# Latent attention: queries of a pair of heads behind the preceding pair's keys

## The chip, the cores and the metric

One core of a Trainium2 chip runs the whole kernel. PE is TensorE, DVE VectorE, ACT ScalarE, POOL GpSimd and SP SyncE; each takes its instructions in the order in which they stand in its queue. ACT and SP also issue DMAs. The metric is the device time of one execution in microseconds; lower is better. Before the change it is 2350.18 us (median of three runs, 2349.92 to 2350.8).

## What is computed

A decoder trunk of two layers over 512 tokens of 1024 channels, in float32. Each layer has three branches beside each other (a state-space mixer, multi-head latent attention, a gated delta net), merges them with gates, and ends with a feed-forward block. The change lies in latent attention:

```python
def mla_mixer(cq, ckv, k_rope, cos, sin, q_norm_g, w_uq, kv_norm_g, w_ukv):
    q = (rmsnorm(cq, q_norm_g) @ w_uq).reshape(Bsz, S, H, MLA_NOPE + MLA_ROPE)
    q_nope, q_pe = jnp.split(q, [MLA_NOPE], axis=-1)
    q_pe = apply_rope(q_pe, cos[:, :, None, :], sin[:, :, None, :])
    kv = (rmsnorm(ckv, kv_norm_g) @ w_ukv).reshape(Bsz, S, H, MLA_NOPE + MLA_V)
    k_nope, v = jnp.split(kv, [MLA_NOPE], axis=-1)
    k_pe = apply_rope(k_rope, cos, sin)
    ...
        sc = (jnp.einsum('bqhd,bkhd->bhqk', qn, k_nope, preferred_element_type=jnp.float32)
              + jnp.einsum('bqhr,bkr->bhqk', qp, k_pe, preferred_element_type=jnp.float32))
        ...
        pr = jax.nn.softmax(sc, axis=-1)
        return jnp.einsum('bhqk,bkhd->bqhd', pr.astype(v.dtype), v)
```

There are 8 heads; a query latent of 512 channels and a key latent of 256; per head 128 channels without and 64 with rotation, and 128 value channels.

## The kernel before

Every float32 product is made of three matmuls: each operand is split into a high part (a cast on ACT) and a low part (a subtraction on DVE), and `mm3` (L181 to L183) adds high times high, high times low and low times high. Names that end in h and l are these parts: whi and wlo of a weight, cqh and cql of the query latent, ckh and ckl of the key latent.

The latent attention of a layer runs like this. `latent` takes the query latent and then the key latent: sums of squares on ACT (L491), a power on POOL (L265), scaling on DVE (L495), transposes on PE into a bank of PSUM (L500), and the eviction into high and low parts with the gain (`split_gain`, L260 on ACT and L261 on DVE). `rope` turns a tile by its angles: four DMAs that swap halves (L513), issued by ACT, then cosine, sine and sum on DVE (L515 to L517). The rotated key goes into kph and kps. Then a loop goes over four pairs of heads. For each pair it makes:
- the queries: weights (casts L552 and L553, low parts L554 and L555), a dense product with the query latent (cq) into three banks, the evictions qh and ql (`head_tiles`, L568 and L569) and qp (L575), the rope of qp, two DMAs that swap the halves of the two heads (L580), and the tiles qps and qpl. Of qps one half is a cast of the rope's sum (L584), the other a cast of what the DMAs of L580 brought (L586).
- the keys and values from the key latent (ck): kh and kl, and the values vh and vl (evicted by `split_act`, L256 on ACT and L257 on DVE), 128 tokens at a time.
- for each head the scores (L617 to L622, of which L620 reads qps), the maximum (L626), the exponential (L629), the division (L630, L631), transposes of the probabilities (L639), their eviction (tiles mix and pt, L256 and L257) and the product with the values (L655 to L657). The result goes into the tiles y.

PSUM has four banks for dense products (acc), three small ones (sm, for scores and transposes) and one for the result of a head (y, named yt in the rows). A scheduler sets the order of each engine's queue when the kernel is built, by dependences, priorities (`tc.high_priority`) and free buffers; the order in which the code is written counts, and buffers of one name are reused in turn. After the first pair the small step sizes of the state-space branch are made (`step_sizes`). In the lists below numbers behind names are those of buffers, and waits names the semaphores an instruction waits for.

Of the kernel before, what the change touches and what calls it, by code (L numbers as in the profile page):

```python
# [11 lines left out]
F32R = mybir.dt.float32r  # L12
# [3 lines left out]
ALU = mybir.AluOpType  # L16
# [4 lines left out]
P = 128  # L21
S = 512
# [37 lines left out]
def hybrid_kernel(ctx, tc, a, out, depth=2, taps=None):  # L60
    nc = tc.nc
    pe, act, dve, pool, sync = nc.tensor, nc.scalar, nc.vector, nc.gpsimd, nc.sync
    uid = itertools.count()

    def mk(pl, shape, dt, tag, bufs=None):
        return pl.tile(shape, dt, tag=tag, name=f"{tag}_{next(uid)}", bufs=bufs)

    def tap(name, ap):
        if taps and name in taps:
            sync.dma_start(taps[name], ap)  # L70

    def f32(ap):
        return ap.bitcast(F32)
# [12 lines left out]
    lp = ctx.enter_context(tc.tile_pool(name="lp", bufs=1))  # L86
# [7 lines left out]
    def y_bank():  # L94
        return mk(ps_sm, [P, 512], F32, "yt", 1)

    def sm_bank():
        return mk(ps_sm, [P, 512], F32, "sm")
# [64 lines left out]
    def weights(w2d, c0, n, K, hold=None):  # L163

        kt = min(1024 // n, K // P)
        step = 512 // n
        for k0 in range(0, K // P, kt):  # L170
            raw = mk(wp, [P, kt * n], F32, "wraw", 2)
            sync.dma_start(raw.rearrange("p (k n) -> p k n", n=n),
                           w2d[k0 * P : (k0 + kt) * P, c0 : c0 + n].rearrange("(k p) n -> p k n", p=P))
            for q in range(0, kt, step):
                hi, lo = split_half(raw[:, q * n : (q + step) * n], hold and hold[k0 + q])
                v = lambda x: x.rearrange("p (k n) -> p k n", n=n)
                yield k0 + q, v(hi), v(lo)
# [76 lines left out]
    def split_act(hi, lo, src):  # L254
        with tc.high_priority(30):
            act.copy(hi, src)  # L256
            dve.tensor_tensor(lo, src, f32(hi), ALU.subtract)  # L257
# [78 lines left out]
    for ly in range(depth):  # L336
# [5 lines left out]
        sconv_b, g_n1, g_ssd, g_q, g_kv, g_gdn, g_n2 = 0, 12, 20, 28, 32, 34, 35  # L342
# [28 lines left out]
        ps = sm_bank()  # L371
# [113 lines left out]
        def latent(tok, width, gi, nm):  # L485

            nk = width // P
            ss = mk(sp, [P, T], F32, "lss")
            for t in range(T):
                jk = mk(ml, [P, width], F32, "pn3", 2)  # L490
                act.activation(jk, tok[t], AF.Square, accum_out=ss[:, t : t + 1])  # L491
            rs = mk(sp, [P, T], F32, "lrs")
            rsq(rs, ss, 1.0 / width, EPS)
            for t in range(T):
                dve.tensor_scalar(tok[t], tok[t], rs[:, t : t + 1], None, ALU.mult)  # L495
            hs, ls = hilo_tags(ml, nm, nk)
            for k in range(nk):
                ps = sm_bank()
                for t in range(T):
                    pe.transpose(ps[:, t * P : (t + 1) * P], tok[t][:, k * P : (k + 1) * P], ident)  # L500
                split_gain(hs[k], ls[k], ps, col(gi + k))
            return hs, ls
# [1 line left out]
        ck_tok = [mk(lp, [P, 256], F32, "mix", 8) for t in range(T)]  # L504
        dense_T(weights(w_in, O_CKV, 256, D), 256, D, xh, xl, lambda t, ps: act.copy(ck_tok[t], ps))
        cqh, cql = latent(cq_tok, 512, g_q, "cq")
        ckh, ckl = latent(ck_tok, 256, g_kv, "ck")

        def rope(src):

# [20 lines left out]
        for x in pts:  # L531
            pool.memset(f32(x[:, :P]), 0.0)

        qpl = [mk(ml, [P, S], F32R, f"qpl{j}") for j in range(2)]
        for j in range(2):
            pool.memset(f32(qpl[j][64 * (1 - j) : 64 * (1 - j) + 64]), 0.0)

        scale = (128 + 64) ** -0.5
        yh, yl = [None] * KD, [None] * KD
        for hp in range(4):  # L540
            def q_weights():
                for k0 in (0, 2):
                    raw = mk(wp, [P, 768], F32, "wraw", 2)
# [12 lines left out]
                        yield k0 + k, hi.unsqueeze(1), lo.unsqueeze(1)  # L556

            *pq, pp = dense_F(q_weights(), tiles(384), 512, cqh, cql)

            def head_tiles(pss, nm, c=None):  # L560
                res = []
                for ps in pss:
                    hi = mk(ml, [P, S], F32R, nm + "h", 3)
                    lo = mk(ml, [P, S], F32R, nm + "l", 3)
                    if c is None:
                        split_act(hi, lo, ps)
                    else:
                        act.mul(hi, ps, c)  # L568
                        dve.scalar_tensor_tensor(lo, ps, c, f32(hi), ALU.mult, ALU.subtract)  # L569
                    res.append((hi, lo))  # L570
                return res

            qs = head_tiles(pq, "q", scale)
            qp = mk(ml, [P, S], F32, "qp")
            act.mul(qp, pp, scale)  # L575
            qr = rope(qp)
# [1 line left out]
            qd = mk(lp, [P, S], F32, "mix", 8)  # L578
            for i in range(2):
                act.dma_start(qd[64 * i : 64 * i + 64], qr[64 * (1 - i) : 64 * (1 - i) + 64])  # L580
            qps = [mk(ml, [P, S], F32R, f"qps{j}") for j in range(2)]
            for j in range(2):
                half, other = (slice(64 * i, 64 * i + 64) for i in (j, 1 - j))
                act.copy(qps[j][half], qr[half])  # L584
                dve.tensor_tensor(qpl[j][half], qr[half], f32(qps[j][half]), ALU.subtract)
                act.copy(qps[j][other], qd[other])  # L586
            wkv = list(weights(a["mla_w_ukv"][ly], hp * 512, 512, 256))
            with tc.high_priority(30):
                ks = head_tiles(dense_F(wkv, [slice(0, P), slice(256, 256 + P)], 256, ckh, ckl), "k")
# [15 lines left out]
            vcols = lambda w: w.rearrange("p (h n) -> p h n", h=2)[:, :, P:]  # L605
            dense_T(wkv, 256, 256, ckh, ckl, ev, vcols)

            for j in range(2):
                qh, ql = qs[j]
                kh, kl = ks[j]  # L610
                pn = []
                for t in range(T):
                    n = max(256, (t + 1) * P)
                    tok = slice(t * P, (t + 1) * P)
                    ps = sm_bank()
                    o = ps[:, :n]
                    pe.matmul(o, qh[:, tok], kh[:, :n], start=True, stop=False)  # L617
                    pe.matmul(o, qh[:, tok], kl[:, :n], start=False, stop=False)
                    pe.matmul(o, ql[:, tok], kh[:, :n], start=False, stop=False)
                    pe.matmul(o, qps[j][:, tok], kps[:, :n], start=False, stop=False)  # L620
                    pe.matmul(o, qpl[j][:, tok], kph[:, :n], start=False, stop=False)
                    pe.matmul(ps[:, t * P : n], id_b, am_b[:, : n - t * P], start=False, stop=True)  # L622
                    n = (t + 1) * P
                    o = ps[:, :n]
                    mx = mk(sp, [P, 1], F32, "mx", 8)
                    dve.tensor_reduce(mx, o, AX.X, ALU.max, negate=True)  # L626
                    pt_ = mk(ml, [P, (t + 1) * P], F32, f"pn{t}", 2)
                    sm = mk(sp, [P, 1], F32, "sme", 8)
                    act.activation(pt_[:, :n], o, AF.Exp, bias=mx, accum_out=sm)  # L629
                    dve.reciprocal(sm, sm)  # L630
                    dve.tensor_scalar(pt_[:, :n], pt_[:, :n], sm, None, ALU.mult)  # L631
                    pn.append(pt_)
                po = y_bank()
                for kbs in ((0,), (1,), (3, 2)):
                    ps = sm_bank()
                    n = 0
                    for kb in kbs:
                        for t in range(kb, T):
                            pe.transpose(ps[:, n : n + P], pn[t][:, kb * P : (kb + 1) * P], ident)  # L639
                            n += P  # L640
                    if len(kbs) == 1:
                        th = mk(lp, [P, n], F32R, "mix", 8)
                        tl = mk(lp, [P, n], F32R, "mix", 8)
                        split_act(th, tl, ps[:, :n])
                        parts = [(kbs[0], kbs[0] * P, 0)]
                    else:

                        th, tl = pts
                        split_act(th[:, P:], tl[:, P:], ps[:, :n])
                        parts = [(2, 2 * P, 2 * P), (3, 2 * P, 0)]  # L650
                    for kb, c0, c in parts:
                        v_h, v_l = (x[:, kb, :] for x in vs[j])
                        o = po[:, c0:]
                        w = S - c0
                        pe.matmul(o, v_h, th[:, c : c + w], start=kb == 0, stop=False)  # L655
                        pe.matmul(o, v_h, tl[:, c : c + w], start=False, stop=False)
                        pe.matmul(o, v_l, th[:, c : c + w], start=False, stop=kb == T - 1)  # L657
                yh[2 * hp + j], yl[2 * hp + j] = (mk(lp, [P, S], F32R, f"y{e}{2 * hp + j}") for e in "hl")
                split_act(yh[2 * hp + j], yl[2 * hp + j], po)
                tap(f"oT{2 * hp + j}", f32(yh[2 * hp + j]))  # L660
            if hp == 0:
                dec, ndec, beta, dtq, dsk, g24 = step_sizes()
        mp.close()
# [621 lines left out]
```

## Time and profile before

| what | value |
|---|---|
| median of three runs | 2350.18 us |
| the profiled execution | 2350.16 us, its span 2348.4 us, clock 0.999 |
| latent attention, first layer | about 46 to 165 us of the span |
| latent attention, second layer | about 1208 to 1330 us |
| PE busy in 46 to 165 | 114.25 of 119.00 us |
| PE busy in 1208 to 1330 | 116.91 of 122.00 us |

A row of the timeline gives the start, the duration, the engine and line, the operation with its output and input, the shape, and in brackets the engine's idle time ahead of it and what ended that. Durations of PE overlap, since matmuls are pipelined: the distance from one start to the next tells what a matmul costs. A row of waits gives the total, the number of times and the longest.

### The profile page before, as it was taken

The numbers are of one execution on the slowest core, as the hardware profiler recorded it, in microseconds if no ns is written. First come the engines' busy times: TensorE is split into PE (matmuls) and PEld (weight loads), VectorE is DVE, ScalarE is ACT, GpSimd is POOL, SyncE is SP. The second block draws the span as 40 slices with busy tenths as digits, with TensorE's granted clock in tenths as the row PEclk, the third lists the DMA queues.
The fourth block names the chain that finished last, engine by engine and source line by source line (L and its number), as shares of the span: only waits on it lengthen the run. The fifth ranks groups of instructions, "written<-read, shape, count | busy, mean of one in ns | idle before, by whom it ended". The sixth has DMA issues, their size and how long they took to land.

```text
span 2348.4 us, 32069 instructions
## 1 busy us (share of the span) xinstructions
PE 2307.8 (98%) x11972; PEld 1896.2 (81%) x11972; DVE 1607.3 (68%) x3184; ACT 1154.4 (49%) x2305; POOL 58.5 (2%) x76
## 2 busy tenths in 40 slices
PE   8999999999999999999999999999999999999998
PEld 7787788888887888888887887888887878888886
DVE  6776756775675458767757777667766645677668
ACT  5655434533453345545656553444334534555545
POOL 0000000000000000000000000000000000000000
PEclk9999999999999999999999999999999999999999
DMA  4322232252222443233132222323422224333231
GB/s 131 91 64 72 65 97 70 79 149 73 73 63 72 143 150 102 72 125 117 46 100 78 73 72 70 93 65 106 117 81 66 62 81 161 126 111 105 90 108 45
DMA packets 194172, 215.16 MB, mean 92 GB/s; under 512 B 32352, under 2 KB 153696, under 8 KB 194016
## 3 DMA queue, kind: packets, MB, share of 16 engines
q1 hardware_dynamic: 190496, 207.87, 29.1%
q10 hardware_dynamic: 3520, 5.25, 0.9%
q8 instruction: 94, 1.54, 0.3%
q14 instruction: 62, 0.51, 0.1%
HBM read 200.50 MB, written 7.34 MB: 89 GB/s over the span
## 4 chain that ended last, share of the span: by engine, by line
PE 90%; DVE 5%; DMA 2%; ACT 1%; POOL 1%; issue 1%; SPq 0%; ACTq 0%; DVEq 0%; POOLq 0%
PE acc L181 23%; PE acc L182 23%; PE acc L183 23%; PE sm L183 2%; PE sm L181 2%; PE sm L182 2%; PE sm L735 1%; DVE wlo L160 1%; PE sm L639 1%; PE yt L182 1%; PE yt L181 1%; PE yt L183 1%; PE sm L1000 1%; PE sm L296 1%; PE sm L461 1%
## 5 line engine op out<-in xcount | busy, mean ns | idle before, releaser
L160 DVE TENSOR_TENSOR wlo<-wraw,whi 128x512 fp32r<-128x512 f32 x552 | 377.9, 688 | 401.8 <-ACT whi L159 391.8
L159 ACT CAST whi<-wraw 128x512 fp32r<-128x512 f32 x552 | 341.9, 621 | 623.6 <-PE acc L182 407.9
L181 PE MATMUL acc<-xh,whi 128*128 128x512 f32 (+1 forms) x1184 | 462.0, 391 | 0.0
L182 PE MATMUL acc<-xl,whi 128*128 128x512 f32 (+1 forms) x1184 | 459.4, 388 | 0.0
L183 PE MATMUL acc<-xh,wlo 128*128 128x512 f32 (+1 forms) x1184 | 459.0, 388 | 0.0
L182 PEld LDWEIGHTS acc<-xl,whi 128*128 128x128 f32 x1184 | 223.0, 188 | 42.5 <-issue 1.0
L183 PEld LDWEIGHTS acc<-xh,wlo 128*128 128x128 f32 x1184 | 222.9, 188 | 41.8 <-issue 0.5
L181 PEld LDWEIGHTS acc<-xh,whi 128*128 128x128 f32 x1184 | 222.8, 189 | 41.7 <-issue 0.5
L181 PE MATMUL acc<-yh,whi 128*128 128x512 f32 x384 | 153.1, 402 | 0.0
L182 PE MATMUL acc<-yl,whi 128*128 128x512 f32 x384 | 152.3, 397 | 0.0
L183 PE MATMUL acc<-yh,wlo 128*128 128x512 f32 x384 | 151.4, 394 | 0.0
L183 PE MATMUL acc<-whi,xl 128*128 128x512 f32 (+1 forms) x384 | 144.0, 375 | 0.0
L181 PE MATMUL acc<-whi,xh 128*128 128x512 f32 (+1 forms) x384 | 143.9, 376 | 0.0
L182 PE MATMUL acc<-wlo,xh 128*128 128x512 f32 (+1 forms) x384 | 143.4, 373 | 0.0
L676 DVE SCALAR_TENSOR_TENSOR cva<-acc,pc,cva 128x511 f32<-128x511 f32 (+2 forms) x168 | 120.2, 743 | 16.7 <-ACT cva L672 9.5
L159 ACT CAST whi<-wr 128x512 fp32r<-128x512 f32 x128 | 79.5, 621 | 68.3 <-PE acc L183 32.7
L181 PE MATMUL acc<-whi,yh 128*128 128x512 f32 x256 | 99.7, 390 | 0.0
L183 PE MATMUL acc<-whi,yl 128*128 128x512 f32 x256 | 99.7, 389 | 0.0
L182 PE MATMUL acc<-wlo,yh 128*128 128x512 f32 x256 | 99.6, 389 | 0.0
L160 DVE TENSOR_TENSOR wlo<-wr,whi 128x512 fp32r<-128x512 f32 x128 | 85.8, 685 | 12.6 <-ACT whi L159 12.1
L182 PEld LDWEIGHTS acc<-yl,whi 128*128 128x128 f32 x384 | 72.2, 188 | 16.1 <-issue 1.9
L181 PEld LDWEIGHTS acc<-yh,whi 128*128 128x128 f32 x384 | 71.6, 188 | 16.8 <-ACT yh L260 2.3
(409 smaller groups left out, 4597.9 us busy)
## 6 DMA issues: line engine op xcount, KB each, us to landing
wraw<-in_w_in_dram SPq DMA_DIRECT2D x148, 512.0 KB, 3.6
wraw<-in_w_up_dram SPq DMA_DIRECT2D x64, 512.0 KB, 3.7
wr<-in_w_down_dram SPq DMA_DIRECT2D x32, 1024.0 KB, 5.0
wraw<-in_w_mla_out_dram SPq DMA_DIRECT2D x16, 512.0 KB, 3.4
wraw<-in_w_ssd_out_dram SPq DMA_DIRECT2D x16, 512.0 KB, 3.4
wraw<-in_w_gdn_out_dram SPq DMA_DIRECT2D x16, 512.0 KB, 3.3
wraw<-in_w_out_dram SPq DMA_DIRECT2D x16, 512.0 KB, 3.7
wraw<-in_mla_w_uq_dram SPq DMA_DIRECT2D x16, 384.0 KB, 3.4
```

The source lines that it names most:

```text
L159: act.copy(hi, raw)
L160: dve.tensor_tensor(lo, raw, f32(hi), ALU.subtract)
L181: pe.matmul(o, ah, bh, start=start, stop=False, skip_group_check=more)
L182: pe.matmul(o, ah, bl, start=False, stop=False, skip_group_check=more)
L183: pe.matmul(o, al, bh, start=False, stop=stop, skip_group_check=more)
L296: pe.transpose(ps[:, j * P : (j + 1) * P], xr[j % 2][:, kk * P : (kk + 1) * P], ident)
L461: pe.matmul(ps, w, cum[1][:, t].rearrange("p i l -> p (i l)"), start=True, stop=True)
L639: pe.transpose(ps[:, n : n + P], pn[t][:, kb * P : (kb + 1) * P], ident)
L676: dve.scalar_tensor_tensor(acc[:, d:], ps[:, : S - d], taps_[3 - d], acc[:, d:], ALU.mult, ALU.add)
L735: pe.matmul(py[:, h * 64 : (h + 1) * 64], e2[h // 4][:, h % 4, :], xd[:, h * 64 : (h + 1) * 64], start=True, stop=True)
L1000: pe.matmul(po[:, h * P : (h + 1) * P], pt_[:, h, :], vn[:, h * P : (h + 1) * P], start=True, stop=True)
```

## The change

The body of the loop is cut into three functions: `queries`, `keys` and `attend`. The order is now queries of the first pair, the key latent, and then for each pair its keys, the next pair's queries, and its attention. So that two pairs' queries can live at once, the odd pairs' tiles use room that is free at that time: tiles of y, and of the query latent for the last pair. The idle halves of their qpl are cleared on POOL each time (4 clearings of 64x512 per layer more), and all these clearings stay in the order of the program. The fourth transposed block of the query latent goes into the bank y instead of a small one. The matmuls are the same in number and size; SP's queue has the same order as before.

```diff
             hs, ls = hilo_tags(ml, nm, nk)
             for k in range(nk):
-                ps = sm_bank()
+                ps = y_bank() if k == 3 else sm_bank()
...
         cqh, cql = latent(cq_tok, 512, g_q, "cq")
-        ckh, ckl = latent(ck_tok, 256, g_kv, "ck")
...
-        qpl = [mk(ml, [P, S], F32R, f"qpl{j}") for j in range(2)]
+        base_qpl = [mk(ml, [P, S], F32R, f"qpl{j}") for j in range(2)]
+        clean = lambda x, j: tc.keep_in_program_order(pool.memset(f32(x[64 * (1 - j) : 64 * (1 - j) + 64]), 0.0))
         for j in range(2):
-            pool.memset(f32(qpl[j][64 * (1 - j) : 64 * (1 - j) + 64]), 0.0)
+            clean(base_qpl[j], j)
...
-        for hp in range(4):
+        def head_tiles(pss, nm, c=None, homes=None):
+            res = []
+            for j, ps in enumerate(pss):
+                hi, lo = homes[j] if homes else (mk(ml, [P, S], F32R, nm + e, 3) for e in "hl")
...
+        y_home = lambda k: [mk(lp, [P, S], F32R, f"y{e}{k}") for e in "hl"]
+        cq_home = lambda k: [mk(ml, [P, S], F32R, f"cq{e}{k}") for e in "hl"]
+
+        def queries(hp):
...
-            qs = head_tiles(pq, "q", scale)
+            qs = head_tiles(pq, "q", scale, [y_home(hp * 2 + j if hp == 1 else 6 + j) for j in range(2)] if hp % 2 else None)
             qp = mk(ml, [P, S], F32, "qp")
             act.mul(qp, pp, scale)
             qr = rope(qp)
...
-            qps = [mk(ml, [P, S], F32R, f"qps{j}") for j in range(2)]
+            if hp % 2:
+                qps, qpl = zip(*((y_home if hp == 1 else cq_home)(k) for k in ((4, 5) if hp == 1 else (2, 3))))
+                for j in range(2):
+                    clean(qpl[j], j)
+            else:
+                qps, qpl = [mk(ml, [P, S], F32R, f"qps{j}") for j in range(2)], base_qpl
             for j in range(2):
                 half, other = (slice(64 * i, 64 * i + 64) for i in (j, 1 - j))
                 act.copy(qps[j][half], qr[half])
                 dve.tensor_tensor(qpl[j][half], qr[half], f32(qps[j][half]), ALU.subtract)
                 act.copy(qps[j][other], qd[other])
+            return qs, qps, qpl
+
+        def keys(hp):
...
+            return ks, vs
+
+        def attend(hp, qs, qps, qpl, ks, vs):
...
+        qq = [queries(0)]
+        ckh, ckl = latent(ck_tok, 256, g_kv, "ck")
+        for hp in range(4):
+            kv = keys(hp)
+            if hp < 3:
+                qq.append(queries(hp + 1))
+            attend(hp, *qq[hp], *kv)
             if hp == 0:
                 dec, ndec, beta, dtq, dsk, g24 = step_sizes()
```

In the new code the lines of queries are L571 to L574 (weights' casts and low parts), L548 and L549 (qh and ql), L580 (qp), L585 (the two DMAs), and L594 to L596 (own half of qps, qpl, other half of qps). The rope is L512 to L516, the scores are L634 to L639, the exponential L646, the transposes of the probabilities L656 and the clearings L531.

The first place is ACT's queue at the first pair of the first layer, where the values are evicted. Before, the eight value evictions (vh) end ahead of the first of the two DMAs L580:

```order
L256 CAST vh_854<-acc_858 128x128
L256 CAST vh_856<-acc_860 128x128 [waits DVE_49]
L552 CAST whi_1172<-wraw_1170 128x256 [waits DMAHW1_49]
L256 CAST vh_856<-acc_861 128x128 [waits DVE_49]
L256 CAST vh_856<-acc_859 128x128 [waits DVE_49]
L256 CAST vh_856<-acc_858 128x128 [waits DVE_49]
L553 CAST whi_1172<-wraw_1170 128x128
L552 CAST whi_1187<-wraw_1170 128x256
L553 CAST whi_1187<-wraw_1170 128x128
L580 DMA mix_811<-mix_807 64x512 [waits DMAHW0_49,DVE_49]
L159 CAST whi_1234<-wraw_1232 128x512 [waits DMAHW6_49,PE_49]
```

Now the row ahead of the DMAs is the third eviction of the first head:

```order
L256 CAST vh_854<-acc_860 128x128 [waits PE_49]
L571 CAST whi_939<-wraw_937 128x256 [waits DMAHW1_49,PE_49]
L585 DMA mix_777<-mix_773 64x512 [waits DMAHW7_49,DVE_49]
L585 DMA mix_777<-mix_773 64x512
L594 CAST qps_162_780<-mix_773 64x512
L594 CAST qps_163_781<-mix_773 64x512
L596 CAST qps_163_781<-mix_777 64x512 [waits DMAHW7_49]
L256 CAST vh_856<-acc_858 128x128 [waits DVE_49]
L596 CAST qps_162_780<-mix_777 64x512 [waits DMAHW1_49]
L256 CAST vh_856<-acc_859 128x128 [waits DVE_49]
L256 CAST vh_854<-acc_861 128x128 [waits PE_49]
```

The two DMAs and the four casts of qps, two of which wait for the DMAs, stand ahead of the rest of the second head's values (vh_856).

The second place is ACT's queue in the attention of the first pair, first layer, from an exponential (pn) to the evictions of transposed probabilities (mix and pt). Before:

```order
L629 ACTIVATE pn_197_911,sme_912<-sm_902,mx_909 128x128 [waits DVE_49]
L629 ACTIVATE pn_201_925,sme_926<-sm_916,mx_923 128x256 [waits DVE_49]
L629 ACTIVATE pn_205_939,sme_940<-sm_930,mx_937 128x384 [waits DVE_49]
L629 ACTIVATE pn_209_953,sme_954<-sm_944,mx_951 128x512 [waits DVE_49]
L568 ACTIVATE qh_1202<-acc_1135 128x512 [waits PE_49]
L568 ACTIVATE qh_1206<-acc_1136 128x512 [waits PE_49]
L256 CAST mix_964<-sm_959 128x512 [waits PE_49]
L256 CAST pt_149_717<-sm_982 128x384 [waits PE_49]
L256 CAST mix_975<-sm_971 128x384
```

Now, from the fourth exponential on:

```order
L646 ACTIVATE pn_234_1054,sme_1055<-sm_1045,mx_1052 128x512 [waits DVE_49]
L585 DMA mix_988<-mix_984 64x512 [waits DVE_49]
L585 DMA mix_988<-mix_984 64x512
L594 CAST yh_216_991<-mix_984 64x512
L594 CAST yh_218_993<-mix_984 64x512
L596 CAST yh_218_993<-mix_988 64x512 [waits DMAHW1_49]
L256 CAST mix_1065<-sm_1060 128x512 [waits PE_49]
L596 CAST yh_216_991<-mix_988 64x512 [waits DMAHW2_49]
L256 CAST mix_1076<-sm_1072 128x384 [waits PE_49]
L256 CAST pt_137_683<-sm_1083 128x384 [waits PE_49]
```

Between exponential and evictions now stand the two DMAs and the four casts of the second pair's qps (which live in the tiles yh_216 and yh_218), with the waits for the DMAs.

The third place is PE's queue where the scores of the second pair's first head begin (first layer). Before:

```order
L183 MATMUL acc_1506<-cqh_122_632,wlo_1542 128x512
L181 MATMUL acc_1611<-ckh_138_682,whi_1603 128x512 [waits DVE_49,Activation_49]
L181 MATMUL acc_1504<-cqh_123_633,whi_1556 128x512
L182 MATMUL acc_1611<-ckl_140_684,whi_1603 128x512
L620 MATMUL sm_1312<-kps_713,qps_281_1224 128x256 [waits Activation_49]
L621 MATMUL sm_1312<-kph_712,qpl_151_721 128x256 [waits DVE_49]
L622 LDWEIGHTS id_b_77
```

Now:

```order
L182 MATMUL acc_1318<-cql_127_637,whi_1368 128x512
L183 MATMUL acc_1318<-cqh_123_633,wlo_1369 128x512
L634 MATMUL sm_1413<-kh_1260,yh_208_969 128x256 [waits PE_49]
L635 MATMUL sm_1413<-kl_1261,yh_208_969 128x256
L636 MATMUL sm_1413<-kh_1260,yl_209_970 128x256
L637 MATMUL sm_1413<-kps_679,yh_216_991 128x256
L638 MATMUL sm_1413<-kph_678,yl_217_992 128x256 [waits Pool_49]
```

The product with qps (L620) stood first here, behind key products that lie further ahead, and waits for ACT; now the key products (L634 to L636) stand together with it, the product with qps (L637, in yh_216) has no wait of its own, and the next (L638) has one for POOL's clearing.

More of the change, by code (lines that the diff above doesn't have):

```diff
@@ L532, in hybrid_kernel @@
             pool.memset(f32(x[:, :P]), 0.0)
-        qpl = [mk(ml, [P, S], F32R, f"qpl{j}") for j in range(2)]
+        base_qpl = [mk(ml, [P, S], F32R, f"qpl{j}") for j in range(2)]
+        clean = lambda x, j: tc.keep_in_program_order(pool.memset(f32(x[64 * (1 - j) : 64 * (1 - j) + 64]), 0.0))
         for j in range(2):
-            pool.memset(f32(qpl[j][64 * (1 - j) : 64 * (1 - j) + 64]), 0.0)
+            clean(base_qpl[j], j)
         scale = (128 + 64) ** -0.5
         yh, yl = [None] * KD, [None] * KD
-        for hp in range(4):
+        def head_tiles(pss, nm, c=None, homes=None):
+            res = []
+            for j, ps in enumerate(pss):
+                hi, lo = homes[j] if homes else (mk(ml, [P, S], F32R, nm + e, 3) for e in "hl")
+                if c is None:
+                    split_act(hi, lo, ps)
+                else:
+                    act.mul(hi, ps, c)
+                    dve.scalar_tensor_tensor(lo, ps, c, f32(hi), ALU.mult, ALU.subtract)
+                res.append((hi, lo))
+            return res
+        y_home = lambda k: [mk(lp, [P, S], F32R, f"y{e}{k}") for e in "hl"]
+        cq_home = lambda k: [mk(ml, [P, S], F32R, f"cq{e}{k}") for e in "hl"]
+        def queries(hp):
             def q_weights():
@@ L558, in hybrid_kernel @@
             *pq, pp = dense_F(q_weights(), tiles(384), 512, cqh, cql)
[L560 to L571, printed above, removed]
-            qs = head_tiles(pq, "q", scale)
+            qs = head_tiles(pq, "q", scale, [y_home(hp * 2 + j if hp == 1 else 6 + j) for j in range(2)] if hp % 2 else None)
             qp = mk(ml, [P, S], F32, "qp")
@@ L580, in hybrid_kernel @@
                 act.dma_start(qd[64 * i : 64 * i + 64], qr[64 * (1 - i) : 64 * (1 - i) + 64])
-            qps = [mk(ml, [P, S], F32R, f"qps{j}") for j in range(2)]
+            if hp % 2:
+                qps, qpl = zip(*((y_home if hp == 1 else cq_home)(k) for k in ((4, 5) if hp == 1 else (2, 3))))
+                for j in range(2):
+                    clean(qpl[j], j)
+            else:
+                qps, qpl = [mk(ml, [P, S], F32R, f"qps{j}") for j in range(2)], base_qpl
             for j in range(2):
```

## The prediction

> **What bounds the kernel now.** I read first the busy shares and the chain of the page, then the waits of PE in the two latent attention stages (about 46 to 165 us and 1208 to 1330 us), then the timelines of PE, DVE and ACT there.
>
> ```profile
> span 2348.4 us, 32069 instructions
> PE 2307.8 (98%) x11972; PEld 1896.2 (81%) x11972; DVE 1607.3 (68%) x3184; ACT 1154.4 (49%) x2305; POOL 58.5 (2%) x76
> PE 90%; DVE 5%; DMA 2%; ACT 1%; POOL 1%; issue 1%; SPq 0%; ACTq 0%; DVEq 0%; POOLq 0%
> ```
>
> PE is busy for 98% of the span and carries 90% of the chain. The change keeps every matmul, so it can only move PE's idle time. What there is of it in the first layer's stage, and then in the second's (total us, times, longest):
>
> ```profile
> PE sm L620 <- ACT qps L586: 1.4, 2, 0.8
> PE sm L500 <- DVE cql L261: 1.2, 1, 1.2
> PE sm L500 <- DVE mix L495: 1.0, 1, 1.0
> PE acc L181 <- DVE vl L257: 0.6, 1, 0.6
> PE acc L181 <- ACT cqh L260: 0.3, 1, 0.3
> ...
> PE sm L620 <- ACT qps L586: 1.9, 1, 1.9
> PE acc L181 <- DVE vl L257: 1.5, 2, 0.8
> PE sm L500 <- DVE mix L495: 1.0, 1, 1.0
> PE acc L181 <- ACT cqh L260: 0.3, 1, 0.3
> ```
>
> That is 4.5 us and 4.7 us. Were all of it gone, the gain would be 9.2 us of 2350, 0.39%. So the forecast is a balance of small waits: those removed against those that the new order makes. 0.2%, 4.7 us, is about what a measurement of this kernel can tell from no change.
>
> **The change, part by part.** The profiled execution took 2350.16 us, 0.02 under the median of the runs, and 1.76 more than its span; the sum is made against 2350.16.
>
> *Removed.* The queries' rotary halves (L586) are now made while the preceding pair is attended to, so the scores no longer wait for them: 1.4 + 1.9 = 3.3 us. In the second layer one value wait lies at a later pair (0.8, the other half of the 1.5) and goes with the order too. Each wait costs a little more than its idle time, because the pipeline of PE refills:
>
> ```profile
> 80.19 0.47 PE L181 MATMUL acc<-cqh,whi 128*128 128x512 f32 x1 [0.65 <-DVE vl L257]
> 80.49 0.40 PE L182 MATMUL acc<-cql,whi 128*128 128x512 f32 x1
> 80.72 0.39 PE L183 MATMUL acc<-cqh,wlo 128*128 128x512 f32 x1
> ...
> 115.83 0.39 PE L182 MATMUL acc<-ckl,whi 128*128 128x512 f32 x1
> 116.80 0.39 PE L620 MATMUL sm<-kps,qps 128*128 128x256 f32 x1 [0.57 <-ACT qps L586]
> ...
> 1240.88 0.47 PE L181 MATMUL acc<-cqh,whi 128*128 128x512 f32 x1 [0.72 <-DVE vl L257]
> ```
>
> Starts of 512-wide matmuls lie 0.23 us apart when nothing is waited for (80.49 to 80.72). From 115.83 to 116.80 are 0.97, that is 0.74 lost where the row says 0.57. With 0.17 for each of the four waits the removed part is 3.3 + 0.8 + 0.7 = **4.8 us**.
>
> *Moved at the start: the first pair.* Today key transposes and key matmuls of the first pair lie between its query matmuls, so the latents' eviction is covered. Afterwards the order is queries, key transposes, keys, first scores, second pair's queries. I walked that order through, with durations of these rows; I end at the start of the second pair's queries, which today is 80.19.
>
> ```profile
> 61.63 2.06 DVE L261 SCALAR_TENSOR_TENSOR cql<-sm,pc,cqh 128x512 fp32r<-128x512 f32 x3
> 68.78 0.75 DVE L261 SCALAR_TENSOR_TENSOR ckl<-sm,pc,ckh 128x512 fp32r<-128x512 f32 x1 [0.37 <-ACT ckh L260]
> 81.06 0.68 DVE L517 TENSOR_TENSOR mix<-mix,mix 128x512 f32<-128x512 f32 x1
> 1222.25 2.07 DVE L261 SCALAR_TENSOR_TENSOR cql<-sm,pc,cqh 128x512 fp32r<-128x512 f32 x3 [0.17 <-ACT cqh L260]
> ...
> 69.15 0.69 ACT L260 ACTIVATE ckh<-sm,pc 128x512 fp32r<-128x512 f32 x1
> 74.78 0.60 ACT L575 ACTIVATE qp<-acc 128x512 f32<-128x512 f32 x1
> 75.41 0.51 ACTq L513 DMA_DIRECT2D mix<-qp  x1
> 77.25 0.60 ACTq L513 DMA_DIRECT2D mix<-qp  x1
> 79.75 0.60 ACT L256 CAST vh<-acc 128x128 fp32r<-128x128 f32 x3
> 81.78 0.50 ACTq L580 DMA_DIRECT2D mix<-mix  x1
> 82.76 0.54 ACTq L580 DMA_DIRECT2D mix<-mix  x1
> 83.34 0.62 ACT L584 CAST qps<-mix 64x512 fp32r<-64x512 f32 x1
> ...
> mix<-qp ACTq DMA_DIRECT2D x32, 64.0 KB, 2.0
> mix<-mix ACTq DMA_DIRECT2D x16, 128.0 KB, 2.3
> DMA to landing us min/median/max: 2.2/2.3/5.6
> ```
>
> The last row is that of L580 alone. The first low half of the query latent is there at 61.63 + 2.06/3 = 62.3, as today; 34 of the 36 query matmuls come after it: 62.3 + 34 x 0.23 = 70.1. ACT then makes qp (0.60): 70.9 with its wait for the last matmul. The first half of the key latent and four swap issues follow; the four take 77.25 + 0.60 - 75.41 = 2.44, up to 73.6 with a start at 71.1. The two key casts (kph, kps) run beside them, as today. Only then comes the second half of the key latent (0.69 and 0.75 on DVE): 75.0. Six matmuls of 0.23, the key's eviction (0.6 on ACT) and two on DVE (0.68 each) bring the rope's sum to between 78.8 and 79.3, against 81.06 + 0.68 = 81.7 today. It is earlier, but PE is now not busy with queries while it runs.
>
> Behind the sum stand two swap issues on ACT (0.5 each), two casts, and the copy of the first landed half: 79.3 + 2.3 = 81.6, and 0.62 to 82.2. Behind that copy, in ACT's order, stand the four value evictions of the second head (0.60 for three, and a low half of each on DVE), and one of their banks is the one that the second pair's queries start in. So these start at about 82.5 to 82.9 where PE is through its own work at about 80.2: a new wait of 2.3 to 2.7 in place of 0.65. Against 80.19 the loss is 2.3 to 2.7, and I take **2.5**. Nothing else hides it: the scores of the second head need the same banks' successors. The second layer has the same distance from the query latent to this place (80.19 - 61.63 = 18.6; 1240.88 - 1222.25 = 18.6), so again 2.5: **5.0** for both. Two steps of 0.3 less each give 1.9 per layer, a longest landing (5.6) gives 5.8.
>
> *Moved inside the pairs.* Between the exponentials of a pair, ACT now issues four swaps, two more, and waits for landings before evictions of the transposed probabilities (mix<-sm), which the value products of PE need; the key's low halves stand behind the rope's steps on DVE. Today none of this lies there, so the trace doesn't price it. Lower end 0: PE has the key and value matmuls of the next pair to fill in, some 24 of 0.23 us (5.5 us). Upper end: one pair of the three pays the four issues and one landing whole, 2.44 + 2.3 = 4.7 a layer. The nearest rows are L586's own waits, where such a landing meets PE with as much to fill in: 0.6 to 1.9 at a time, 1.4 and 1.9 a layer. I take 2.4 per layer, halfway between the ends and a little over these: **4.8**.
>
> *Added, at no cost.* Four memsets of 64x512 per layer go to POOL. Two of them took 1.09 us, and POOL idles for 125 us in this stage:
>
> ```profile
> 14.31 1.09 POOL L536 MEMSET qpl<- 64x512 f32 x2
> 191.06 0.53 POOL L431 MEMSET wk<- 128x512 f32 x1 [125.24 <-DVE pn L631]
> ```
>
> If POOL were behind a wait for the last pair's tiles (which held the query latent), the attention of the pair before would hide the 0.55. The fourth bank for transposes (y) lets all 16 run at once; it removes the 1.2 for cql at that transpose, but the low product that follows needs the same cql, so the walk above already holds what remains of it. SP's order of loads is the same, at nothing.
>
> The sum: 2350.16 + 5.0 + 4.8 - 4.8 = 2355.2 us, slower by 0.21%.
>
> **Rivals.**
> - *The first pair pays, the pairs stay smooth.* Key and value matmuls fill the new waits inside the pairs: 5.0 - 4.8 = +0.2, 2350.4. For it: the 24 matmuls; against: they themselves stand in PE's order and can't be pulled ahead.
> - *The rope is in time (the other side).* If the rope's sum is there 2 us sooner, at 76.8, the copy is done by 80.0 and the evictions by 80.5, and the first pair loses nothing; with the pairs smooth too, only the removal is left: 2345.4, and 2341.0 if the 9.2 us go whole. The point from which it decides is the fourth swap, issued by 71.5 instead of 73.6 (2.0 to landing, then sin, other casts and sum on DVE). Against it: qp itself can't be ready before 70.7.
> - *Long landings.* The median landing of L580 is 2.3, the longest 5.6. If the first pair's landings are such in one layer, that is 3.3 more, 2358.5; in both, 2361.8. [...] At the start of the program, behind 10.25 us of idle PE, the starts of 512-wide matmuls lie 0.43 apart up to 18.8 and 0.23 after 19.2, nine us into the work:
>
> ```profile
> 17.96 0.63 PE L181 MATMUL acc<-whi,xh 128*128 128x512 f32 x1
> 18.39 0.63 PE L182 MATMUL acc<-wlo,xh 128*128 128x512 f32 x1
> ...
> 19.17 0.39 PE L181 MATMUL acc<-whi,xh 128*128 128x512 f32 x1
> 19.40 0.39 PE L182 MATMUL acc<-wlo,xh 128*128 128x512 f32 x1
> ```
>
> A wait of 1.9 shows no such pace behind it in the rows of the stage, so I price a 2.5 us wait without it; one of 5.8 would be new here. [...]
>
> **How the numbers follow.** The likeliest case is the sum, chance 0.50; with 0 to 4.7 per layer inside the pairs its own range is 2351 to 2360, and somewhat over half of it (0.31) is over 4.7 us, the rest (0.19) within. The smooth pairs have 0.18, no change. The rope in time has 0.18, of which 0.16 is faster by over 4.7 us, since 2345.4 is its mildest form, and 0.02 within. Long landings have 0.14, slower. Together: faster 0.16, within 0.2% 0.39, slower 0.45. The range leaves out the lower part of the rope in time (0.1) and the upper part of the long landings (0.1): 2344 to 2361.
>
> **What would show it.** Right: PE waits no more for L596's copies at the score matmuls of the later pairs; in both layers the second pair's first query matmul waits 2 to 3 us for a value eviction (vl L257), and that eviction for L596 on ACT; and waits of about 1 us for evictions of the transposed probabilities at one or two pairs. PE's busy sum stays at 2308. Wrong: that first query matmul without a wait over 1 us (then the rope was in time), or one over 4 us (a landing); no POOL row may release PE. The prediction falls altogether if the time changes outside the two stages, or if the first scores wait for another thing than the evictions, such as the 512-wide weights' casts that now stand among ACT's rotary work.

## The result, and the profile after

The changed kernel takes 2379.05 us (median of four runs, 2378.83 to 2379.32) against 2350.49 before: a ratio of 1.0122, 95% interval 1.011 to 1.0134. It is slower by 28.6 us; forecast were 5, and the range ended at 2361. The busy shares and the chain of the page after:

```profile
span 2377.4 us, 32066 instructions
PE 2316.7 (97%) x11972; PEld 1904.7 (80%) x11972; DVE 1610.1 (68%) x3184; ACT 1156.9 (49%) x2305; POOL 62.4 (3%) x84
PE 86%; DVE 6%; DMA 3%; ACT 2%; issue 1%; POOL 1%; ACTq 1%; SPq 0%; DVEq 0%; POOLq 0%
```

PE has the same 11972 matmuls, but they were busy 8.9 us longer (2307.8 before), and the span grew by 29.0. So there are two losses: idle time, and matmuls that ran slower. PE's waits in the first layer's stage (40 to 190 us), and the first three rows for the second layer's:

```profile
PE yt L672 <- ACT mix L256: 4.4, 3, 2.8
PE acc L181 <- DVE vl L257: 3.8, 2, 2.6
PE acc L181 <- DVE kl L257: 3.6, 3, 2.5
...
PE acc L181 <- DVE vl L257: 4.5, 2, 2.6
PE yt L672 <- ACT mix L256: 4.4, 3, 2.8
PE acc L181 <- DVE kl L257: 3.5, 3, 2.3
```

No row for qps is left: the waits that the change was to remove are gone. In their place stand three new kinds: a value (vl) at the second pair's first queries, a key's low half (kl) and the evictions of transposed probabilities (mix) inside the pairs. Added up, the rows of waits in both stages (44 to 250 and 1205 to 1440) give 29.6 us of idle PE, against 10.2 before. Of the 19.4 that came, 17.3 lie inside the pairs (kl and mix) and 6.2 belong to vl (8.3 against 2.1, all of it at the first pair now); 3.3 for qps and 0.8 of other rows went.

The clock is the other loss. Slices of 1 us, with PE, PEld, DVE, ACT and POOL busy (instructions), the granted clock, the DMA share and GB/s:

```profile
88.00:89.00 1.00, 1.00 (x3) 0.76 (x3) 0.31 (x1) 0.62 (x1) 0.00 (x0) 0.50 0.83 187
90.00:91.00 1.00, 1.00 (x6) 0.82 (x5) 0.00 (x0) 0.30 (x1) 0.00 (x0) 1.00 0.00 0
```

PE is granted half its clock from 82.8 to 89.6 and from 171.5 to 175. One minus the clock, summed over all slices of the two stages, is 5.1 us per layer, 10.2 in all; before, no slice of them is below full clock. 19.4 more idle and 10.2 of clock make 29.6, against the 29.0 by which the span grew; a little of the slow time is idle at once (the wait of 1.19 that ends at 85.48 lies in a stretch of half clock).

### The profile page after: what moved, and what is told of

Read it like the earlier page. It is cut to its first block, busy times and chain, and to the rows that moved or that the text cites. A ratio compares the mean times of both kernels' runs of the same rounds, so it can differ in the third digit from the quotient of the medians.

```text
span 2377.4 us, 32066 instructions
## 1 busy us (share of the span) xinstructions
PE 2316.7 (97%) x11972; PEld 1904.7 (80%) x11972; DVE 1610.1 (68%) x3184; ACT 1156.9 (49%) x2305; POOL 62.4 (3%) x84
## 3 DMA queue, kind: packets, MB, share of 16 engines
q1 hardware_dynamic: 190496, 207.87, 27.6%
## 4 chain that ended last, share of the span: by engine, by line
PE 86%; DVE 6%; DMA 3%; ACT 2%; issue 1%; POOL 1%; ACTq 1%; SPq 0%; DVEq 0%; POOLq 0%
PE acc L181 22%; PE acc L182 22%; PE acc L183 22%; PE sm L183 2%; PE sm L181 2%; PE sm L182 2%; PE sm L760 1%; DVE wlo L160 1%; DMA mix<-qp 1%; PE yt L182 1%; PE yt L181 1%; PE yt L183 1%; PE sm L1025 1%; PE sm L461 1%; PE sm L1006 1%
## 5 line engine op out<-in xcount | busy, mean ns | idle before, releaser
L160 DVE TENSOR_TENSOR wlo<-wr,whi 128x512 fp32r<-128x512 f32 x128 | 85.9, 687 | 12.5 <-ACT whi L159 11.7
```

Of the source, the lines that this page charges most:

```text
L160: dve.tensor_tensor(lo, raw, f32(hi), ALU.subtract)
```

## The experiments

All are built from the changed kernel and compared with the kernel before in the same batch.

**Whose place costs: the key latent's or the queries'?** Two runs undo one each.

```diff
 own_order
         for hp in range(4):
+            if hp:
+                qq.append(queries(hp))
             kv = keys(hp)
-            if hp < 3:
-                qq.append(queries(hp + 1))
             attend(hp, *qq[hp], *kv)
 ck_first
-        qq = [queries(0)]
         ckh, ckl = latent(ck_tok, 256, g_kv, "ck")
+        qq = [queries(0)]
```

> The changed kernel with each later pair's queries back in front of its own keys (queries, keys, attend); the key latent still comes behind the first queries. By the rows of the changed kernel the first pair costs some 6 us more per layer than before (waits of 2.6 and 1.2 to 1.9 for value evictions, and 16 matmuls at half pace behind them) and the three later pairs some 8 per layer. Theory 1, in-order queues: ACT's and DVE's waits for landings stand ahead of what feeds PE, both at the first pair and inside the pairs: 2350.5 + 12 = about 2362, and no kl or mix wait over 1 us. Rival 2, the place of the key latent alone costs all: stays at 2379. Rival 3, the moved queries alone cost all: 2350 to 2352.

> The changed kernel with the key latent back ahead of the first queries; queries still behind the preceding pair's keys. Theory 1 (both places cost): the two waits for vl at the start of the second pair's queries and the half pace go, the kl and mix waits stay: about 2379 - 12 = 2367. Rival 2 (place of the key latent alone): 2350 to 2352. Rival 3 (moved queries alone): 2379.

Measured: own_order 2366.5 us (1.0073, interval 1.0057 to 1.0089), ck_first 2361.2 (1.0051, 1.0035 to 1.0066). Both places cost, so rivals 2 and 3 fall. The waits of PE in the first layer's stage, own_order first:

```profile
PE sm L637 <- ACT qps L596: 2.7, 2, 1.6
PE acc L181 <- DVE vl L257: 2.6, 1, 2.6
...
PE yt L672 <- ACT mix L256: 4.4, 3, 2.8
PE acc L181 <- DVE kl L257: 2.9, 3, 1.3
```

With the queries back, the value wait of 2.6 stays and the kl and mix waits go, but qps is waited for again; with the key latent back, vl is gone and kl and mix stay. own_order came out 4.5 us above the 2362 of theory 1, ck_first 5.8 below its 2367.

**Is it the landing?** The prediction had ACT wait for a landed DMA ahead of the value evictions. This run moves only the copies of landed halves, to the head of the attention that uses them:

```diff
 copies_late
             for j in range(2):
                 act.copy(qps[j][half], qr[half])
                 dve.tensor_tensor(qpl[j][half], qr[half], f32(qps[j][half]), ALU.subtract)
-                act.copy(qps[j][other], qd[other])
+            def landed():
+                for j in range(2):
+                    act.copy(qps[j][other], qd[other])
...
         def attend(hp, qs, qps, qpl, landed, ks, vs):
+            landed()
```

> The changed kernel; only the two copies per pair that wait for the landed swaps (L596) are written at the head of the attention that uses them, so ACT's queue has the value evictions and the evictions of probabilities ahead of them. Theory 1: the waits for vl (2.6 and 1.2) and for mix (2.8) go, with the half pace behind them; the waits for kl behind DVE's rope product (2.5 and 0.9 per layer) stay: some 6 + 5 less per layer, about 2357. Rival 4, the landings themselves have become long (4.8 instead of 2.3) and meet PE wherever the copies stand: over 2370, the wait now at the score product with qps.

Measured: 2370.9 us (1.0094, 1.0078 to 1.011). Both expectations missed: the time is not 2357, and though it is over the 2370 of rival 4, no score product waits for qps, which was to be its sign. The timelines of PE, ACT and DVE in this run:

```profile
82.83 0.77 PE L181 MATMUL acc<-cqh,whi 128*128 128x512 f32 x1 [2.62 <-DVE vl L257]
...
79.11 1.15 ACTq L585 DMA_DIRECT2D mix<-mix  x2
80.31 1.25 ACT L594 CAST qps<-mix 64x512 fp32r<-64x512 f32 x2 [0.85 <-DVE wlo L573]
81.59 0.77 ACT L256 CAST vh<-acc 128x128 fp32r<-128x128 f32 x4
...
80.96 1.40 DVE L595 TENSOR_TENSOR qpl<-mix,qps 64x512 fp32r<-64x512 f32 x2 [1.00 <-ACT qps L594]
82.39 0.88 DVE L257 TENSOR_TENSOR vl<-acc,vh 128x128 fp32r<-128x128 f32 x4
```

The wait of 2.6 is the same without the copies. From 79.11 to 81.56 ACT only issues two DMAs and casts two halves, and DVE then makes qpl until 82.36; the evictions vh and vl stand behind. So the first wait is made of ACT's and DVE's own rotary work that stands ahead of the evictions; no landing of the two DMAs L585 is in it. What did go is the second wait at that place (1.2 in the changed kernel), and with it, in the first layer, one of its two stretches of half clock.

**Which queue?** act_late writes the swaps by heads (L585), the casts, qpl and copies behind the own pair's keys, and leaves the rope's products and sum where the change put them. tail_late moves those products and the sum, too.

```diff
 act_late, in queries
             qr = rope(qp)
+            def halves():
...
+                return qps, qpl
+            return qs, halves
 tail_late, in queries (swap: the four DMAs of the rope alone)
-            qr = rope(qp)
+            sw = swap(qp)
+            def tail():
+                qr = rope(qp, sw)
...
+                return qps, qpl
+            return qs, tail
 the loop of tail_late; act_late's has halves for tail
             kv = keys(hp)
+            qs, tail = qq[hp]
+            rot = tail()
             if hp < 3:
                 qq.append(queries(hp + 1))
-            attend(hp, *qq[hp], *kv)
+            attend(hp, qs, *rot, *kv)
```

> The changed kernel; the rope's sum on DVE stays where the change put it, ahead of the preceding pair's attention, but the two swaps by heads and the four casts and copies that follow it (L585, L594 to L596) are written behind the own pair's keys. Theory 5: ACT's queue is the place of the waits for vl (2.6 and 1.2) and for mix (0.8, 0.8, 2.8), by the work ahead of the evictions (two issues of 0.58 and two casts of 0.63) as by the landing; DVE's queue is that of the waits for kl (2.5 and 0.9): the kl waits stay, the others go: 2350 - 4 + 7 = about 2353. Rival 6: DVE's queue is the place of nearly all, since the sum and qpl stand ahead of vl and kl: over 2368.

> The changed kernel; the whole rear part of the rope of a pair (products, sum, the two swaps by heads, casts and copies) is written behind that pair's keys instead of ahead of the preceding pair's attention; matmuls, evictions and the first four swaps stay as changed. Theory 1: nothing on ACT or DVE waits for a landing ahead of what feeds PE, so all new waits go: 2350 plus or minus 3. Rival 4 (long landings): over 2365, PE waiting for qps at the scores as before the change, but longer.

Measured: act_late 2358.6 us (1.0033, 1.002 to 1.0045), tail_late 2345.6 (0.9983, 0.9973 to 0.9993), faster than both kernels. act_late is 5.6 us above theory 5's 2353, tail_late 1.4 below the range of theory 1. PE's timeline in act_late (first layer) and then all waits over 0.3 us of tail_late's first stage:

```profile
98.08 0.38 PE L181 MATMUL acc<-whi,ckh 128*128 128x256 f32 x1 [1.37 <-DVE kl L257]
158.37 0.39 PE L181 MATMUL acc<-whi,ckh 128*128 128x256 f32 x1 [1.17 <-DVE kl L257]
162.75 0.50 PE L676 MATMUL yt<-mix,vh 128*128 128x512 f32 x1 [1.34 <-DVE mix L257]
...
PE acc L182 <- DVE cql L261: 1.4, 1, 1.4
PE acc L181 <- ACT ckh L260: 1.3, 2, 0.9
PE acc L181 <- DVE kl L257: 0.8, 1, 0.8
```

In act_late 0.2 us per layer is left of the waits for vl and 2.1 of the 5.1 for mix, with one of 1.3 that I had not expected (mix's low half, on DVE); the waits for kl stay (3.4 and 3.1 in the two layers, against 3.6 and 3.5). So the work behind the rope's sum (issues, casts, copies and qpl) carries the first pair and most of mix, and the products and the sum on DVE carry kl. That is theory 5 by place, but not cleanly by queue: act_late moves a subtraction of DVE (qpl, L595) along with ACT's work, and in copies_late vl stood directly behind that subtraction. What ACT's share of the first wait is by itself was not tried. Together the two places are the whole loss: tail_late, with the same moves of queries and latent, keeps of these waits only 0.8 for kl and 0.2 for mix per layer.

**What the moved queries are worth then.** own_tail is tail_late with the loop of own_order.

> tail_late, but each later pair's queries again in front of its own keys, as before the change: it tells what moving the queries is worth by itself once the rear of the rope stands behind the keys. Theory 9, the move takes away the waits for qps (3.3 us of idle time before, some 4 with refills): they come back, 2345.6 + 4 = about 2349.5. Rival 10, the gain of tail_late comes from the rear of the rope standing later (ACT and DVE freer), not from the moved queries: 2345 to 2347.

Measured: 2359.4 us (1.0035, 1.0022 to 1.0048). Both expectations were too low: own_tail is 8.3 us over the kernel before of its batch, tail_late 4.4 under that of its own, so with the rope's rear behind the keys the queries' early place is worth 12.7 us. Part of it is in the waits of own_tail, first stage and then second (the row for cva, a tile of another branch, is the same in both):

```profile
PE sm L647 <- ACT qps L604: 1.6, 1, 1.6
...
PE acc L181 <- DVE cva L713: 2.0, 1, 2.0
PE sm L647 <- ACT qps L604: 1.5, 1, 1.5
```

The waits of both stages add up to 14.5 us, against 6.5 in tail_late, and 1.7 of clock come on top: 9.7 of the 12.5 by which the spans differ. Some 3 I have not placed.

**The clock.** fill lets PE work through the first wait, with products that nobody reads:

```diff
             kv = keys(hp)
+            if hp == 0:
+                spare = y_bank()
+                for _ in range(11):
+                    pe.matmul(spare, kv[1][0][0][:, 2, :], qq[0][0][0][0], start=True, stop=True)
```

> The changed kernel plus 11 matmuls of 512 columns per layer whose result nobody reads, placed by their input (the third value block) where PE waits for the second pair's first bank. The wait of 2.6 us is then filled, the second pair's queries start no sooner. Theory 7, the clock: the 16 query matmuls behind that wait run 0.43 apart only because PE was idle; filled, they run 0.23 apart: 16 x 0.2 = 3.2 less per layer, about 2372.5, though the kernel does more. Rival 8, the slow pace comes from something else there (the landing's traffic, evictions): 2379 to 2380.

Measured: 2378.3 us (1.0117, 1.0103 to 1.0131), no change in time that can be told. PE's timeline in the first layer:

```profile
79.51 2.68 PE L686 MATMUL yt<-qh,vh 128*128 128x512 f32 x11
83.45 0.39 PE L182 MATMUL acc<-cql,whi 128*128 128x512 f32 x1
83.68 0.40 PE L183 MATMUL acc<-cqh,wlo 128*128 128x512 f32 x1
86.20 0.47 PE L181 MATMUL acc<-cqh,whi 128*128 128x512 f32 x1 [1.90 <-DVE vl L257]
87.32 0.63 PE L182 MATMUL acc<-cql,whi 128*128 128x512 f32 x1
87.75 0.63 PE L183 MATMUL acc<-cqh,wlo 128*128 128x512 f32 x1
```

Filled, the first queries run 0.23 apart (83.45 to 83.68) where they ran 0.43 apart in the changed kernel, so idle time was the reason, at this first stretch. But the second wait (1.2 before, 1.9 here) stayed, and behind it PE is slow from 87.0 to 90.5 (0.43 apart). One minus the clock adds up to 5.1 us here, 10.2 in the changed kernel. Idle PE is 3.1 less (26.5 against 29.6), and the 22 added matmuls cost 22 x 0.23 = 5.1, which leaves 3.1 of gain; the span is 1.9 shorter, the median 0.7, in a batch whose kernel before is 0.9 slower. I had not counted the added work, nor that the second wait would bring on a stretch of its own.

**Small parts of the change.** bank_sm has the fourth transposed block in a small bank again, unpinned leaves the clearings' place to the scheduler, and tail_ck is tail_late with the key latent back in front.

```diff
 bank_sm
-                ps = y_bank() if k == 3 else sm_bank()
+                ps = sm_bank()
 unpinned
-        clean = lambda x, j: tc.keep_in_program_order(pool.memset(...))
+        clean = lambda x, j: pool.memset(...)
 tail_ck: the loop of tail_late, with the first lines of ck_first
```

> The changed kernel with the fourth transposed block of the query latent back in a small bank. The wait of 1.2 for cql at that transpose comes back in part; PE waits 1.45 for the same cql anyway: 2379 to 2380, no change that can be told.

> The changed kernel with the clearings left to the scheduler. POOL is idle for over 100 us in both stages, no row of POOL ends a wait of PE in the changed kernel: 2379 plus or minus 2. If the pinned clearings held up the scores: below 2375.

> tail_late with the key latent back ahead of the first queries: the waits for ckh (0.4 and 0.9 per layer) and their refills go, a wait of about 0.55 for mix comes back: 2345.6 - 2 = about 2343.5. If the key latent's place does something good behind other work (for the rope, whose sum comes sooner): 2345 to 2347.

Measured: bank_sm 2378.7 us (1.0121, 1.0105 to 1.0136), unpinned 2382.9 (1.0136, 1.0119 to 1.0153), tail_ck 2346.1 (0.9979, 0.9971 to 0.9988). By itself neither the bank nor the pinning moves the time by what can be told: the intervals overlap that of the changed kernel, though unpinned is 1.9 us over the upper end of what was expected. The equal time of bank_sm has another make-up: the wait of 1.2 for cql came back in the first layer, vl's waits are gone, and in both layers transposes of the key latent wait 3.1 us, the longest wait of this run (first layer):

```profile
73.26 1.94 PE L500 MATMUL sm<-ct,mix 128*128 128x128 f32 x8 [3.10 <-DVE mix L495]
```

tail_ck ties with tail_late, 2.6 us above the 2343.5 expected: what it takes from the waits for ckh comes back as waits for mix, qps and kl of 0.4 to 1.5 us.

**All runs in one table.** Idle is the sum of PE's waits in both stages, clock the sum of one minus the granted clock over their slices, both from the profiled execution and in us; the fourth column is idle less the 10.2 of before, plus clock, and the last what the span grew by.

| kernel | idle | clock | both, against before | span, against before |
|---|---|---|---|---|
| before | 10.2 | 0 | | |
| the change | 29.6 | 10.2 | 29.6 | 29.0 |
| unpinned | 30.7 | 10.2 | 30.7 | 31.0 |
| bank_sm | 27.6 | 12.0 | 29.4 | 26.8 |
| fill | 26.5 | 5.1 | 21.4 (26.5 with 5.1 of added work) | 27.1 |
| copies_late | 23.7 | 6.8 | 20.3 | 19.5 |
| own_order | 17.7 | 8.5 | 16.0 | 16.4 |
| ck_first | 20.0 | 1.7 | 11.5 | 10.0 |
| act_late | 16.2 | 1.7 | 7.7 | 9.1 |
| own_tail | 14.5 | 1.7 | 6.0 | 6.8 |
| tail_late | 6.5 | 0 | -3.7 | -5.7 |
| tail_ck | 7.1 | 0 | -3.1 | -6.7 |

The two sums follow the span within 4 us over a reach of 38, so idle time and clock are the whole account, but for a few us.

## Why the prediction was wrong, point by point

**Removed, 4.8: right in kind.** No score product waits for qps after the change. On its own the removal could not be timed, since each run that keeps it changes other waits.

**The first pair, 5.0: right in place and start, too short behind it.** The rows of the changed kernel in the first layer, PE, ACT and DVE, and the long landing from the chain:

```profile
82.49 0.52 PE L181 MATMUL acc<-cqh,whi 128*128 128x512 f32 x1 [2.63 <-DVE vl L257]
83.23 0.63 PE L183 MATMUL acc<-cqh,wlo 128*128 128x512 f32 x1
83.66 0.63 PE L181 MATMUL acc<-cqh,whi 128*128 128x512 f32 x1
85.48 0.77 PE L181 MATMUL acc<-cqh,whi 128*128 128x512 f32 x1 [1.19 <-DVE vl L257]
...
78.76 1.15 ACTq L585 DMA_DIRECT2D mix<-mix  x2
79.96 1.26 ACT L594 CAST qps<-mix 64x512 fp32r<-64x512 f32 x2 [0.85 <-DVE wlo L573]
81.24 0.62 ACT L596 CAST qps<-mix 64x512 fp32r<-64x512 f32 x1
84.11 0.61 ACT L596 CAST qps<-mix 64x512 fp32r<-64x512 f32 x1 [2.09 <-DMA mix<-mix]
...
77.79 0.68 DVE L516 TENSOR_TENSOR mix<-mix,mix 128x512 f32<-128x512 f32 x1
80.61 1.40 DVE L595 TENSOR_TENSOR qpl<-mix,qps 64x512 fp32r<-64x512 f32 x2 [1.00 <-ACT qps L594]
...
79.30 4.79 DMA mix<-mix
```

The rope's sum is done at 78.5 (forecast 78.8 to 79.3), and the second pair's queries start at 82.49 (82.5 to 82.9), 2.30 later than before. But the step "the copy of the first landed half" was the wrong cause: that copy ran at 81.24 without a wait, behind issues and casts, and DVE's qpl kept vl back as long (until 82.01). copies_late has the same wait without the copy. That the time fits is luck: the two issues and two casts took from 78.76 to 81.22, about as long as the landing of 2.3 that I had put there. I stopped the walk at the first bank. The second bank's eviction stands behind the second copy, and its landing took 4.79 us instead of 2.3: another 1.19 (1.86 in the second layer). Together the waits for vl grew by 6.2 us, where the forecast took 0.8 off at the later pair and added 5.0. The long landing was a rival, counted only in the first place, at 0.14.

**Inside the pairs, 4.8: the step that failed.** Each layer loses 8.7 and 8.6 us there (kl 3.6 and 3.5, mix 4.4 and 0.7 each), not 2.4, and the upper end of 4.7 was too low. I let one pair of three pay and let the next pair's keys hide the rest. All three pay, and at both queues. In the first pair of the changed kernel, on ACT, DVE and PE, and the DMA on the chain:

```profile
95.72 2.48 ACTq L512 DMA_DIRECT2D mix<-qp  x4
97.58 4.42 DMA mix<-qp
102.03 0.69 DVE L515 TENSOR_TENSOR mix<-mix,sinT 128x512 f32<-128x512 f32 x1 [1.65 <-DMA mix<-qp]
103.83 0.68 DVE L257 TENSOR_TENSOR kl<-acc,kh 128x512 fp32r<-128x512 f32 x1
104.57 0.39 PE L181 MATMUL acc<-whi,ckh 128*128 128x256 f32 x1 [2.46 <-DVE kl L257]
```

DVE stands still for the fourth swap, which was issued at 97.58 and landed at 102.00, and the eviction of the key that frees PE's bank stands behind it. At the third pair PE waits its longest, 2.84, for an eviction of probabilities behind ACT's casts and copies, and two casts of weights, where no landing is waited for (ACT's timeline, then PE's):

```profile
167.21 0.61 ACT L594 CAST cqh<-mix 64x512 fp32r<-64x512 f32 x1
168.49 1.24 ACT L596 CAST cqh<-mix 64x512 fp32r<-64x512 f32 x2
169.64 0.57 ACT L256 CAST mix<-sm 128x512 fp32r<-128x512 f32 x1
...
170.27 0.50 PE L672 MATMUL yt<-mix,vh 128*128 128x512 f32 x1 [2.84 <-ACT mix L256]
```

That the key products fill such waits was the error: they had already been done, or needed the very bank that was held.

**The clock, priced at nothing for a wait of 2.5.** This is the other failed step, 10.2 us. I priced such a wait without half pace, by rows of the stage that showed none behind 1.9. The changed kernel goes to half clock (0.50 granted) behind 2.63, and again behind 2.84, each time for 3.4 us or twice that; behind 2.46 (104.57) and 2.31 (1281.63) it does not (1.00), and in fill it came behind a wait of 1.90 (86.20). So "PE's busy sum stays at 2308", a sign of being right, failed: it is 2316.7. The slow rows that I had, at the start of the program, are no example of it by the profile: in the kernel before, the granted clock is 1.00 in every slice from 10 to 21 us. What besides a wait brings such a stretch on, no run shows.

**Chances.** The sign had 0.45, and the sum of faster and unchanged 0.55. Both kinds of loss had been named, but the time lies outside the range because each place was priced once: one landing, one pair, no clock.

## What to carry to other kernels

Work moved ahead in a program carries its whole train into the in-order queues of the helper engines (here 17.3 us of PE's waits for kl and mix, and 8.3 for vl). Each eviction that frees a bank for PE must be looked up there by what now stands ahead of it: issues, casts and waits for a DMA alike, at every bank and every pass of the loop. Move early only what PE itself does (here the products, their evictions and the first four swaps), and write the rest behind the evictions: that made the same change 0.17% faster (0.07 to 0.27) instead of 1.2% slower. On PE, price the clock as well: in these runs waits of 1.3 to 3.1 us cost 1.7 or 3.4 us on top at some places, and nothing at others.

## What the runs showed of the hardware

- Half clock came in stretches of 3.4 us, two of them at times in one, with 1.70 or 1.71 us lost in each: the changed kernel lost 5.12 us per layer, three stretches (82.8 to 89.6 is two); copies_late 3.40 and 3.41, two each; tail_late none.
- The length of a wait alone does not tell whether one comes. In ck_first the same wait brings it in one layer only (PE's timeline, first and second layer):

```profile
162.10 0.50 PE L672 MATMUL yt<-mix,vh 128*128 128x512 f32 x1 [2.84 <-ACT mix L256]
1328.35 0.67 PE L672 MATMUL yt<-mix,vh 128*128 128x512 f32 x1 [2.84 <-ACT mix L256]
```

Its clock is full around 162 and half from 1328.5 to 1332. In act_late a wait of 1.3 at 1328.4, with one of 0.7 four us ahead, was followed by such a stretch as well, in the second layer alone.
- Swaps of 64 to 128 KB that mostly land in 2.0 to 2.3 us took 3 to 4.8 at one place per pair of the changed kernel; the kernel before has such landings at other places, up to 5.6. At that of 79.30 and that of 97.58 a weight load of 512 KB was issued by SP within 0.3 us; that the load is the cause wasn't tried.
